# Layer 1's attention with the two query halves in the two row halves of the TensorE array

## The chip, the cores and the metric

The kernel runs on one NeuronCore of one Trainium2 chip, as one launch. The metric is the device time of that launch in microseconds (us), the median of several runs. Inside the core, five engines work side by side, each through its own instructions in order and with semaphores between them: TensorE (PE in the profile; its weight loads are listed apart as PEld), VectorE (DVE), ScalarE (ACT), GpSimd (POOL) and SyncE (SP), which here issues nearly all DMAs. Products are written to PSUM, eight banks of 512 float32 on each of 128 partitions.

## What is computed

Two layers of a transformer-like backbone over 1024 latent tokens and 256 context tokens of width 1024, batch 1, in float32. Layer 0 is grouped-query attention, layer 1 (the last one) multi-head latent attention with 16 heads. Only layer 1's attention is touched by the change. Cut to what matters, for each head, with 64 "nope" columns, 32 rotary columns that all heads share on the key side, and all 1280 keys:

```
s = (einsum("qd,kd->qk", q_nope, k_nope) + einsum("qr,kr->qk", q_rope, k_rope)) * 96 ** -0.5
p = softmax(s, axis=-1)
o = p @ v                      # 1024 queries x 64
y = (o * silu(g)) @ w_out      # all heads together, then x + gate * y
```

## The kernel before

**Precision.** Operands that need float32 accuracy are split into a high part (float32r, rounded) and a low part (what is left). A product is then the sum of high x high, high x low and low x high. For layer 1 the parts of queries and keys lie in DRAM: `q1h`, `q1l` (per head 96 rows: 64 nope, 32 rotary) and `k1h`, `k1l` (64 nope rows per head), `kr1h`, `kr1l` (32 rotary rows for all heads).

**The `Attention` class** serves both layers; each layer hands in a dictionary `ops` with its own functions. A *unit* is one head of latent queries (layer 0 has four more units for the context queries). Layer 1 has 16 units. A unit works through ten *key tiles* of 128 keys:

- `do_scores` (L422, L424): the scores of 128 keys (partitions) against 1024 queries go to a PSUM tile `st` of two banks, 512 queries in each. In layer 1 `l1_scores` gives three operand pairs, each used for both query halves: six products with 96 or 97 rows. The 97th row subtracts a shift for each query: the keys' row is -1, the queries' row (`crow`) is the row's maximum. ScalarE then writes `p`, the exponential, to SBUF.
- Between the products, `one_more` slips in the *maxima* of a later unit (`maxima`, `do_max`, L362 to L369): a product of high parts alone, 128 queries against 512 latent keys, or two products of 128 queries against 256 context keys, into a PSUM tile `mx` of one bank, and a VectorE reduction of that bank. A unit has 16 latent steps and 4 context steps; two steps come with each key tile.
- When a unit's maxima are complete, `do_shift` lines up a turn, which is run after the ten score tiles (`run_turns`): a transpose on TensorE, a copy on VectorE (L384), and a DMA that puts the row into its place beside the queries (L385).
- `add_up` (L445, POOL) and `pair_sum` (L431, DVE) sum the tiles of `p` for the softmax's denominator. `total` (L500 to L506) finishes that sum for the unit before, in the PSUM bank of that unit's `av`.
- `do_av` (L458): the product with V for all ten key tiles, two products of 64 columns for each, one for each query half, in the two column halves of the array. `p` and V are plain float32, so each is two instructions. `finish` copies the result out (L479).

`run` writes down this order for TensorE, VectorE and ScalarE by hand (`manual_schedule`); SP's and POOL's instructions are put in order by the framework. `start_unit` (from `run`, two units ahead) calls the layer's `load`: in layer 1 `l1_load` (L1382 to L1388), six DMAs and a memset of the -1 row, into `KH`, `KL`, `QH`, `QL` with three buffers each. PSUM during the loop: two banks `mx`, two tiles `st` of two banks, two banks `av`.

**Around it.** Before the loop the last eight gate slices of layer 1 run (`gate_slice`, 24 products each, L92 to L94); from the fourth slice on, six maxima steps come with each of four slices, 24 in all, ordered by the framework. `open_early` opens the pools for keys, queries and `mx` before the gate slices, `open_late` the others after them, in memory that the gate's operands leave. Then `run(24, 2, ...)`, then the output projection.

## Time and profile before

| what | value |
|---|---|
| runs | 1738.92, 1737.24 and 1739.38 us; median 1738.92 |
| the profiled execution, first to last instruction (span) | 1736.6 us, 2.3 us under the median |
| granted TensorE clock, mean | 0.997 |
| layer 1's attention loop | about 1197 to 1642 us from the span's start |
| gate slices with maxima before it | about 1168 to 1197 us |
| output projection after it | about 1642 to 1737 us |

The profile is one execution. Matmuls are pipelined: a matmul row's duration (0.39 us for 512 columns) reaches over its drain, so what a product costs TensorE is read from the distance of starts or from the chain of waits, not from the duration. Rows with "x2" or more are runs of like instructions merged, and their time is that of the whole run. A row's bracket tells how long the engine had been idle and who ended that. The chain of waits follows the work that ended last back from the end. The lines themselves stand where the prediction uses them.

### The profile page before, as it was taken

The page shows a single profiled execution, that of the slowest core. Times are in us where ns is not written, and L with a number is a line of the kernel's source. Part 1 is how long each engine was busy: PE and PEld are TensorE (multiplying, and loading weights), DVE is VectorE, ACT ScalarE, POOL GpSimd, SP SyncE. Part 2 cuts the span into 40 slices and gives each one's busy share as a digit, 9 for nine tenths or more (in the row PEclk, how much of TensorE's full clock was granted, in tenths as well). Part 3 has the DMA queues.
Part 4 walks back from the last instruction along what each step waited for, and adds up shares of the span by engine and source line. Part 5 has one row for each costly group of instructions (what it writes and reads, how often), then busy time and mean ns, then how long its engine had stood idle before and what let it go on. Part 6 is the DMA issues. An engine that isn't in the chain of part 4 may idle for free. (4 is left out here: it accounts for less than half of the span.)

```text
span 1736.6 us, 23794 instructions
## 1 busy us (share of the span) xinstructions
PE 1703.1 (98%) x8548; PEld 1232.5 (71%) x8548; DVE 1068.4 (62%) x1807; ACT 644.5 (37%) x943; POOL 979.5 (56%) x657
## 2 busy tenths in 40 slices
PE   8999999999999999999989999999999999999998
PEld 5776778776655665558878798978666666657587
DVE  3765651368777877625575667756676767667231
ACT  4632221134544544433244633332343443434310
POOL 2763430237888897752344644443587878777511
PEclk9999999999999999999999999999999999999999
DMA  9457854432332422156434857685434443441452
GB/s 326 156 160 235 265 167 136 133 98 55 100 91 71 116 66 74 44 145 189 137 94 132 238 163 199 181 234 162 104 88 118 108 104 91 111 112 43 118 162 73
DMA packets 211901, 234.33 MB, mean 135 GB/s; under 512 B 20680, under 2 KB 157880, under 8 KB 211784
## 3 DMA queue, kind: packets, MB, share of 16 engines
q1 hardware_dynamic: 211360, 232.71, 47.2%
q8 instruction: 67, 1.10, 0.3%
q14 instruction: 50, 0.41, 0.1%
q10 hardware_dynamic: 424, 0.11, 0.0%
HBM read 158.98 MB, written 73.63 MB: 134 GB/s over the span
## 5 line engine op out<-in xcount | busy, mean ns | idle before, releaser
L363 DVE TENSOR_REDUCE m<-mx 128x1 f32<-128x512 f32 x512 | 351.5, 691 | 203.6 <-PE mx L362 201.5
L424 ACT ACTIVATE p<-st 128x1024 f32<-128x1024 f32 x328 | 335.3, 1024 | 219.5 <-PE st L422 185.1
L445 POOL TENSOR_TENSOR acp<-acp,p 128x1024 f32<-128x1024 f32 x128 | 305.7, 2388 | 8.7
L458 PE MATMUL av<-p,v 128*64 128x512 f32 x1312 | 289.9, 595 | 0.0
L458 PEld LDWEIGHTS av<-p,v 128*64 128x64 f32 x1312 | 90.8, 137 | 181.0 <-issue 178.6
L445 POOL TENSOR_TENSOR acp<-p 128x1024 f32<-128x1024 f32 x34 | 81.3, 2391 | 168.3 <-ACT p L424 167.9
L445 POOL TENSOR_TENSOR acp<-acp,acd 128x1024 f32<-128x1024 f32 x60 | 141.5, 2358 | 22.2 <-DVE acd L431 19.4
L431 DVE TENSOR_REDUCE acd<-p 128x512 f32<-128x1024 f32 x124 | 144.6, 1219 | 7.7 <-ACT p L424 7.7
L135 POOL TENSOR_TENSOR wb<-wraw,wa 128x512 fp32r<-128x512 f32 (+3 forms) x73 | 95.5, 1324 | 90.6 <-ACT wa L156 90.0
L92 PE MATMUL mm<-wa,hh 128*128 128x512 f32 (+2 forms) x336 | 127.3, 379 | 1.7 <-ACT hh L787 1.7
L422 PE MATMUL st<-QH,KL 96*128 96x512 f32 x320 | 123.5, 392 | 0.0
L94 PE MATMUL mm<-wa,hl 128*128 128x512 f32 (+2 forms) x336 | 121.3, 361 | 1.4 <-DVE hl L790 1.4
L93 PE MATMUL mm<-wb,hh 128*128 128x512 f32 (+2 forms) x336 | 120.9, 360 | 0.0
L479 ACT COPY os<-av 128x512 f32<-128x512 f32 x36 | 21.1, 586 | 252.9 <-PE av L458 173.5
L369 DVE TENSOR_REDUCE m<-mx 128x2 f32<-128x512 f32 x144 | 99.3, 692 | 25.3 <-PE mx L367 24.4
L92 PE MATMUL y<-wa,oh 128*128 128x512 f32 (+1 forms) x296 | 114.1, 386 | 0.0
L93 PE MATMUL y<-wb,oh 128*128 128x512 f32 (+1 forms) x296 | 113.6, 384 | 0.0
L94 PE MATMUL y<-wa,ol 128*128 128x512 f32 (+1 forms) x296 | 113.6, 384 | 0.0
L422 PE MATMUL st<-QA,KA 128*128 128x512 f32 x336 | 106.6, 399 | 0.7 <-ACT p L424 0.7
L422 PE MATMUL st<-QB,KB 65*128 65x512 f32 x336 | 105.5, 395 | 0.0
L362 PE MATMUL mx<-KA,QA 128*128 128x512 f32 x256 | 102.4, 405 | 1.2 <-DVE m L363 1.0
L362 PE MATMUL mx<-KH,QH 96*128 96x512 f32 x256 | 102.3, 401 | 0.0
(232 smaller groups left out, 3423.4 us busy)
## 6 DMA issues: line engine op xcount, KB each, us to landing
mraw<-in_l_w_mod SPq DMA_DIRECT2D x64, 256.0 KB
wraw<-in_l_w_in SPq DMA_DIRECT2D x28, 512.0 KB
rb<-rrow SPq DMA_DIRECT2D x72, 128.0 KB
mraw<-in_l_w_mod SPq DMA_DIRECT2D x16, 512.0 KB
sgd<-gth SPq DMA_DIRECT2D x32, 256.0 KB
QA<-q0h SPq DMA_DIRECT2D x32, 256.0 KB
wraw<-in_l_w_out SPq DMA_DIRECT2D x16, 512.0 KB
sg<-sgd SPq DMA_DIRECT2D x64, 128.0 KB
```

What stands on the lines that cost most here:

```text
L92: pe.matmul(ps, lhsT=lh(k), rhs=rh(k), start=first and i == 0, stop=False)
L93: pe.matmul(ps, lhsT=lh(k), rhs=rl(k), start=False, stop=False)
L94: pe.matmul(ps, lhsT=ll(k), rhs=rh(k), start=False, stop=last and i == len(ks) - 1)
L135: eng.tensor_sub(lo, a, b)
L362: pe.matmul(m, lhsT=s["mq"][:, i * P:(i + 1) * P], rhs=s["mk"][:, n * 512:(n + 1) * 512], start=True, stop=True)
L363: dve.reduce_max(s["m"][:, i, n:n + 1], m, axis=AX.X)
L369: dve.reduce_max(s["m"][:, 2 * i:2 * i + 2, 2 if u["kind"] == "lat" else 0], m.rearrange("p (a b) -> p a b", a=2), axis=AX.X)
L422: pe.matmul(ps[:, n * 512:(n + 1) * 512], lhsT=lh, rhs=rf(n), start=(j == 0), stop=(j == len(prods) - 1))
L424: act.activation(p, ps, AF.Exp, scale=self.ops["scale"])
L431: dve.reduce_sum(t[:, ns], p2.rearrange("p a n -> p n a")[:, ns, :], axis=AX.X)
L445: pool.tensor_add(t, a, b)
L458: pe.matmul(s["av"][64 * n:64 * n + 64, :], lhsT=s["v"][:, kt, u["vc"]:u["vc"] + 64], rhs=p[:, n * 512:(n + 1) * 512], start=kt == kts[0], ...
```

## The change

A constant `HALVES = (False, True)` switches a second form of the attention on for layer 1 alone. (The diff also carries functions for layer 0, which are not called.)

- **Scores** (`scores_by_halves`, `l1_scores` with `n`): query half 0 lives on partitions 0 to 63, half 1 on partitions 64 to 127, so a product of one half has 64 rows and lies in one row half of the array. Keys are held twice, once in each half. The sum over 96 columns and three precision parts is cut into five steps of 64 rows (the last of 33), issued for the two halves in turn: high x high, low x high and high x low of the nope part; then 32 + 32 rows with the rotary keys' high and low parts against the queries' high part twice; then 32 rows of rotary high against the queries' low part with the shift row as the 33rd.
- **Maxima** (`max_parts`, `next_maxima`, `side_by_side`): the same 16 + 4 steps a unit, each of two products of 64 rows (nope, rotary) for one query half. Two steps, one of each half, go with a key tile: half 0's ahead of its scores, half 1's after three of its scores. A latent step is two parts, taken in turn with the other half's products; a context step issues its four products of 256 columns at once (`part_ctx`).
- **PSUM**: three banks `mx`, two tiles `st`, one bank `av`; `total` takes an `mx` tile.
- **Loads** (`l1_load_halves`): `KH`, `QH`, `QR` with three buffers when a unit is started, eight DMAs; `rest` loads `KL`, `QL`, `QS` with two buffers, six DMAs, for unit t+2 after the last scores of unit t. `KR` is filled once in `open_early`, `KS` with its -1 rows in `open_late`. The shift row goes out in two DMAs, and its SBUF tile has one buffer instead of two, in layer 0 too. The pool of the gate slices before the loop has two buffers instead of four.

The diff, cut:

```
+HALVES = (False, True)
...
-            self.ps_m = st.enter_context(tc.tile_pool(name=f"psm{l}", bufs=2, space=PSUM, side="right", reuse_waits="tile"))
+            self.ps_m = st.enter_context(tc.tile_pool(name=f"psm{l}", bufs=3 if HALVES[l] else 2, space=PSUM, side="right", reuse_waits="tile"))
+            if HALVES[l]:
+                self.ops["open"](self, st)
...
+                bufs = 1 if HALVES[l] and name == "ps_o" else 2
...
+        def max_parts(self, u, step):
...
+            def part(j):
+                if j == 0:
+                    held["m"] = self.ps_m.tile([P, 512], F32, name="mx", tag="mx")
+                pairs = self.ops["maxima"](s, half)
+                q, k = pairs[j]
+                for t, ks, cs in spans:
+                    pe.matmul(held["m"][:, cs], lhsT=q[:, t * P:(t + 1) * P], rhs=k[:, ks], start=j == 0, stop=j == len(pairs) - 1)
+                if j == len(pairs) - 1:
+                    dve.reduce_max(s["m"][:, i, n:n + 1], held["m"], axis=AX.X)
+
+            def part_ctx():
+                held["m"] = self.ps_m.tile([P, 512], F32, name="mx", tag="mx")
+                m = held["m"]
+                pairs = self.ops["maxima"](s, half)
+                for t, ks, cs in spans:
+                    for j, (q, k) in enumerate(pairs):
+                        pe.matmul(m[:, cs], lhsT=q[:, t * P:(t + 1) * P], rhs=k[:, ks], start=j == 0, stop=j == len(pairs) - 1)
+                dve.reduce_max(s["m"][:, 2 * i:2 * i + 2, 2 if u["kind"] == "lat" else 0],
+                               m.rearrange("p (a b) -> p a b", a=2), axis=AX.X)
+
+            if kind == "ctx":
+                return half, [part_ctx] + [lambda: None] * (self.ops["mparts"] - 1)
+            return half, [lambda j=j: part(j) for j in range(self.ops["mparts"])]
...
-                r = self.sm.tile([8, P], F32R, name="crow", tag="crow", bufs=2)
+                r = self.sm.tile([8, P], F32R, name="crow", tag="crow", bufs=1)
...
+                    for n in range(2):
+                        sp.dma_start(raw(s["crow"][n]), raw(r[4 * n:4 * n + 4, :]))
...
+            if "rest" in s and self.started < 2:
+                s.pop("rest")()
+            if HALVES[self.l]:
+                if lat:
+                    self.todo += [(u, ("lat", i + 4 * a, n)) for i in range(4) for n in range(2) for a in range(2)]
+                self.todo += [(u, ("ctx", i + 2 * a, 0)) for i in range(2) for a in range(2)]
...
+        def side_by_side(*streams):
+
+            for t in range(max(map(len, streams))):
+                for stream in streams:
+                    if t < len(stream):
+                        stream[t]()
...
+            if HALVES[self.l]:
+                steps = self.next_maxima(upto, limit)
+                self.side_by_side(*([f for half, parts in steps if half == a for f in parts] for a in range(2)))
+                return
...
+        def scores_by_halves(self, u, kt, p, steps):
+
+            s = self.state[id(u)]
+            ps = self.ps_s.tile([P, 1024], F32, name="st", tag="st")
+            prods = [self.ops["scores"](s, kt, n) for n in range(2)]
+            last = len(prods[0]) - 1
+
+            def product(j, n):
+                lh, rh = prods[n][j]
+                pe.matmul(ps[:, n * 512:(n + 1) * 512], lhsT=lh, rhs=rh, start=j == 0, stop=j == last)
+
+            streams = [[lambda j=j, n=n: product(j, n) for j in range(last + 1)] for n in range(2)]
+            for half, parts in steps:
+                at_ = (last + 2) // 2 if half else 0
+                streams[half][at_:at_] = parts
+            self.side_by_side(*streams)
+            act.activation(p, ps, AF.Exp, scale=self.ops["scale"])
...
-                t = s["av"] if u is not self.units[-1] else self.ps_m.tile([P, 512], F32, name="mx", tag="mx")
+                t = s["av"] if u is not self.units[-1] and not HALVES[l] else self.ps_m.tile([P, 512], F32, name="mx", tag="mx")
...
+                            if HALVES[self.l]:
+                                count += 2
+                                self.scores_by_halves(u, kt, ps[i], self.next_maxima(count, t + 1 + ahead))
...
+                        if end and t + 2 < self.started:
+                            self.state[id(self.units[t + 2])].pop("rest", lambda: None)()
...
+    def l1_open(at, st):
+        at.KR = st.enter_context(tc.tile_pool(name="rope1", bufs=1, **right)).tile([P, NT], F32R, name="KR")
+        for n in range(2):
+            sp.dma_start(raw(at.KR[64 * n:64 * n + 32, :]), kr1h)
+            sp.dma_start(raw(at.KR[64 * n + 32:64 * n + 64, :]), kr1l)
+
+    def l1_open_late(at, st):
+        at.KS = st.enter_context(tc.tile_pool(name="rope1s", bufs=1, reuse_waits="tile")).tile([P, NT], F32R, name="KS")
+        for n in range(2):
+            pool.memset(raw(at.KS[64 * n + 32:64 * n + 33, :]), -1.0)
+            sp.dma_start(raw(at.KS[64 * n:64 * n + 32, :]), kr1h)
+
+    def l1_load_halves(u, at):
...
+        halves = [(64 * n, slice(512 * n, 512 * n + 512)) for n in range(2)]
+        for b, cs in halves:
+            sp.dma_start(raw(KH[b:b + 64, :]), k1h[h // 2, r, :])
+            sp.dma_start(raw(QH[b:b + 64, :]), q1h[h, 0:64, cs])
+            for o in (0, 32):
+                sp.dma_start(raw(QR[b + o:b + o + 32, :]), q1h[h, 64:96, cs])
+
+        def rest():
+            KL = kp.tile([P, NT], F32R, name="KL", tag="KL", bufs=2)
+            QL = qp.tile([P, 512], F32R, name="QL", tag="QL", bufs=2)
+            QS = qp.tile([P, 512], F32R, name="QS", tag="QS", bufs=2)
+            for b, cs in halves:
+                sp.dma_start(raw(KL[b:b + 64, :]), k1l[h // 2, r, :])
+                sp.dma_start(raw(QL[b:b + 64, :]), q1l[h, 0:64, cs])
+                sp.dma_start(raw(QS[b:b + 32, :]), q1l[h, 64:96, cs])
+            s.update(KL=KL, QL=QL, QS=QS, crow=[QS[b + 32:b + 33, :] for b, _ in halves])
...
+    def l1_maxima(s, n):
+        r = slice(64 * n, 64 * n + 64)
+        return [(s["QH"][r, :], s["KH"][r, :]), (s["QR"][r, :], s["KR"][r, :])]
...
+    def l1_scores(s, kt, n=None):
         ks = slice(kt * P, (kt + 1) * P)
+        if n is not None:
+            r = slice(64 * n, 64 * n + 64)
+            r33 = slice(64 * n, 64 * n + 33)
+            return [(s["KH"][r, ks], s["QH"][r, :]), (s["KL"][r, ks], s["QH"][r, :]), (s["KH"][r, ks], s["QL"][r, :]),
+                    (s["KR"][r, ks], s["QR"][r, :]), (at.KS[r33, ks], s["QS"][r33, :])]
...
-    with tc.tile_pool(name="wkg1", bufs=4, **right) as wkg:
+    with tc.tile_pool(name="wkg1", bufs=2 if HALVES[1] else 4, **right) as wkg:
```

More of the change, by code (lines that the diff above doesn't have):

```diff
@@ L369, in do_max @@
                 dve.reduce_max(s["m"][:, 2 * i:2 * i + 2, 2 if u["kind"] == "lat" else 0], m.rearrange("p (a b) -> p a b", a=2), axis=AX.X)
+        def max_parts(self, u, step):
+            s = self.state[id(u)]
+            kind, i, n = step
+            if kind == "lat":
+                half, spans = i // 4, [(i % 4, slice(n * 512, n * 512 + 512), slice(0, 512))]
+            else:
+                half, spans = i // 2, [(2 * (i % 2) + a, slice(NL, NT), slice(a * 256, a * 256 + 256)) for a in range(2)]
+            held = {}
+            def part(j):
[19 more added lines that the diff above has]
+            return half, [lambda j=j: part(j) for j in range(self.ops["mparts"])]
         def do_shift(self, u):
@@ L1156, in hybrid_kernel @@
         units.insert(pos, ctxu[g])
-    at = Attention(0, units, dict(scale=0.125, load=l0_load, scores=l0_scores, kbufs=2, qbufs=3, vw=256))
+    at = Attention(0, units, dict(scale=0.125, load=l0_load, scores=l0_scores, maxima=l0_maxima, mparts=1, open=l0_open, kbufs=2, qbufs=3, vw=256))
     stE = ExitStack()
@@ L1402, in hybrid_kernel @@
                               kts=list(range(TT))))
-    at = Attention(1, units, dict(scale=float(96 ** -0.5), load=l1_load, scores=l1_scores,
+    at = Attention(1, units, dict(scale=float(96 ** -0.5), load=l1_load, scores=l1_scores, maxima=l1_maxima, mparts=2, open=l1_open, open_late=l1_open_late,
                                   kbufs=3, qbufs=3, vw=128))
```

97 lines of the change are left out of this document (84 added, 13 removed).

## The prediction

> **What bounds the kernel now.** I read the page's totals first, then the busy time by windows, then the chain of waits inside layer 1's attention, then single pieces of that chain.
>
> ```profile
> span 1736.6 us, 23794 instructions
> ...
> PE 1703.1 (98%) x8548; PEld 1232.5 (71%) x8548; DVE 1068.4 (62%) x1807; ACT 644.5 (37%) x943; POOL 979.5 (56%) x657
> ```
>
> ```profile
> 1168.00:1197.00 29.00, 29.00 (x129) 22.78 (x128) 18.50 (x30) 3.53 (x6) 2.54 (x2) 1.00 0.72 206
> 1197.00:1642.00 445.00, 445.00 (x2092) 285.85 (x2090) 291.14 (x419) 179.59 (x187) 324.43 (x161) 1.00 0.39 97
> ```
>
> The two windows are the end of the gate stage and the attention loop of layer 1. In the loop TensorE is busy in all 445 us at full granted clock (1.00), VectorE in 291, GpSimd in 324, ScalarE in 180, the DMA engines in 0.39. The chain agrees that nothing but TensorE's own order sets the pace:
>
> ```profile
> by line: PE st L422 50.7%; PE av L458 29.8%; PE mx L362 13.9%; PE mx L367 3.5%; PE av L500 1.8%; PE mx L382 0.4%; PE mm L94 0.1%
> ```
>
> So time saved on TensorE in this loop is saved from the span, until another engine is late. The change touches the scores (st) and the maxima (mx), not the product with V (av). Pieces of the chain in order of time:
>
> ```profile
> 1207.26 0.23 PE mx L362
> 1207.49 0.70 PE st L422 x3
> 1208.20 0.25 PE mx L367 x2
> 1208.44 0.70 PE st L422 x3
> ...
> 1215.76 8.73 PE av L458 x40
> ```
>
> One product of 512 columns takes a slot of 0.232 us (0.70 / 3), one of 256 columns 0.12 (0.25 / 2). A key tile is six score products and two steps of the maxima: 8 x 0.232 = 1.855 us, or 1.87 where the steps are those over the context keys (4 products of 256 columns). How many of each kind:
>
> ```profile
> L363 DVE TENSOR_REDUCE m<-mx 128x1 f32<-128x512 f32 x236 | 163.2, 691 | 110.3 <-PE mx L362 109.9
> L369 DVE TENSOR_REDUCE m<-mx 128x2 f32<-128x512 f32 x60 | 41.5, 692 | 14.7 <-PE mx L367 14.7
> L424 ACT ACTIVATE p<-st 128x1024 f32<-128x1024 f32 x160 | 163.8, 1024 | 143.4 <-PE st L422 118.3 <-DVE m L369 12.5 <-DVE m L363 11.4
> ```
>
> Two reductions stand in a key tile: 236 / 2 = 118 latent tiles, 60 / 2 = 30 context tiles, and of 160 tiles 12 have none (the last units), at 6 x 0.232 = 1.39 us.
>
> **The change, part by part.**
>
> *Scores.* Six products of 512 columns become ten of 64 (once 33) rows, in pairs that sit in different row halves and write different banks. If a pair takes the slot of one product, that is five slots. No row of this trace shows two row halves at work. The nearest is two column halves, the product with V:
>
> ```profile
> L214 PE MATMUL tp<-modrow,fold x8: 591/591/592, 131.1 to 238.8; 128*2 128x512 f32 x8
> 131.13 1.02 PE L214 MATMUL tp<-modrow,fold 128*2 128x512 f32 x2
> ```
>
> L214 is two passes of 512 float columns with no partner: 1.02 - 0.591 = 0.43 us from start to start. The 40 passes of av, in pairs of column halves, take 8.73 us: 0.437 a pair. There a pair costs what one costs alone. I therefore take **0.232 us for a pair of row halves**, the slot of the same float32r product. Bounds: below, 0.437 / 2 = 0.218 (the av stream at the same number of columns; float32r's own extra over it would vanish). Above, the weights: each product of a pair has its own load of 128 columns, and the closest thing to two loads in a slot is the pair of 256-column products, 0.25 us.
>
> A weight load starts now together with the product before it, on the same rows, and is over before that product's slot is:
>
> ```profile
> 1403.66 0.39 PE L422 MATMUL st<-QH,KL 96*128 96x512 f32 x1
> 1403.67 0.19 PEld L362 LDWEIGHTS mx<-KH,QH 96*128 96x128 f32 x1
> 1403.89 0.39 PE L362 MATMUL mx<-KH,QH 96*128 96x512 f32 x1
> ```
>
> So I count no load beside the slot. [...]
>
> With 0.232: a latent tile is 7 slots (two products of a maximum in one half beside two score products in the other), 1.62 us, so 0.232 x 118 = **-27.4**. A tile without maxima saves one slot: 12 x 0.232 = **-2.8**. A context tile is different: `part_ctx` issues its four 256-column products in one go in one half, and products start in the order of the program in every row here, so three of the four run alone in each half. By hand: 3 x 0.12, then six slots (two score products of half 1 come first, the second beside half 0's first), with the other half's 3 x 0.12 among them: 0.72 + 1.39 = 2.11 us against 1.87, 30 x 0.24 = **+7.2**. Together -23.0. By 0.218 (0.11 for the short ones): -(1.855 - 1.526) x 118 - (1.39 - 1.09) x 12 + (1.97 - 1.87) x 30 = -39.4. By 0.25 (0.125): -0.105 x 118 - 0.14 x 12 + (2.25 - 1.87) x 30 = -2.7.
>
> *What comes next when TensorE is faster.* In a latent tile of 1.62 us VectorE has 2 x 0.691 = 1.38, ScalarE 1.02. Both still fit, VectorE with little room; the third mx buffer keeps it off TensorE's way. GpSimd's 324 us are 20.3 of 27.8 a unit and lose a memset a unit. Cost 0; below 1.4 us a tile VectorE would be the bound.
>
> *The maxima in the gate stage.* 24 steps run there among 128-row products. In the present timeline they stand singly or in twos, about five visits in each of four gate slices, the first and last:
>
> ```profile
> 1168.45 0.70 PE L362 MATMUL mx<-KH,QH 96*128 96x512 f32 x2
> ...
> 1193.77 0.40 PE L362 MATMUL mx<-KH,QH 96*128 96x512 f32 x1
> ```
>
> Afterwards each visit changes the array between whole and halved rows. Such a change can be seen where av ends:
>
> ```profile
> 1420.83 0.14 PEld L458 LDWEIGHTS av<-p,v 128*64 128x64 f32 x2 [0.28 <-issue]
> 1421.78 0.19 PEld L362 LDWEIGHTS mx<-KH,QH 96*128 96x128 f32 x1 [0.81 <-issue]
> 1421.78 0.50 PE L362 MATMUL mx<-KH,QH 96*128 96x512 f32 x1
> 1422.12 0.62 PE L422 MATMUL st<-QL,KH 96*128 96x512 f32 x2
> ```
>
> The first weights come only with the product, and the next product starts 0.34 after it instead of 0.23; with some 0.09 before it, 0.2 us a change. With pairs, ten visits x 2 changes x 0.2 = **+4** (0 if they bunch, 8 for twenty visits). In the loop the number of changes stays: the totals and av are in column tiles already.
>
> *The loads.* `KS` is filled in `open_late`, where memory becomes free with the last gate product, and the fifth step of the first tile needs it. v, loaded at that moment now, shows when:
>
> ```profile
> 1197.10 0.38 SPq L352 DMA_DIRECT2D v<-vd  x1
> 1197.14 0.63 PE L422 MATMUL st<-QL,KH 96*128 96x512 f32 x2
> ...
> 1615.94 1.11 SPq L516 DMA_DIRECT2D rb<-rrow  x2
> 1619.63 1.29 POOL L519 TENSOR_TENSOR rb<-rb,sg 128x512 f32<-128x512 f32 x1 [3.11 <-DMA rb<-rrow]
> ```
>
> rb landed 3.7 us after its first issue. KS, issued at about 1197.5, is there at 1201.2; the fifth step would be due at 1198.5: **+2.7**, once (0 to 5). KL, QL and QS of unit t+2 are asked for at the end of unit t and have a whole unit. A unit issues 14 loads instead of 7 and moves 2.2 MB instead of 1.7 (tile sizes in the code); at 0.4 to 0.7 us an issue (rows here) and a DMA share of 0.39 neither is near its end. The shift row follows them on SP's queue: six issues of about 0.5 us and 1 MB stand ahead of its two.
>
> ```profile
> 1413.02 0.69 SPq L385 DMA_DIRECT2D QH<-crow  x1
> ```
>
> It is issued at 1413.0, its unit's first product starts at 1421.8: nearly 9 us of cover, of which the six issues take 3 and the megabyte some 4 (97 GB/s at a share of 0.39 make 250 GB/s). Cost 0, and if the cover goes, a wait of TensorE at the fifth step of each unit. The totals move from av's bank to an mx buffer, held through the 8.7 us of av, when no maxima run: 0; so av can do with one bank. In layer 0 only one thing changes, one crow buffer instead of two: where two heads end together VectorE waits for a DMA under the cover of av: 0.
>
> **Sum:** -23.0 + 4 + 2.7 = -16.3 us. The execution of the trace (span 1736.6) becomes 1720.3; the median of the runs shown lies 2.3 above that span, so **1722.6 us**.
>
> **The rivals.**
>
> *Weight loads in a row* (slower). If the two loads of a pair follow each other at 0.125, the slot is 0.25: -2.7 + 6.7 = +4.0, **1742.9 us**. It decides from a slot of 0.246, where gain and the 6.7 us cancel. For it: 14 loads in a latent tile, and loads with almost no product between come at 0.10 us each, (0.95 - 0.25) / 7 here:
>
> ```profile
> 192.38 0.95 PE L221 MATMUL tp<-fold,modrow 128*128 128x2 f32 x8
> ```
>
> Against it: av's two loads of 64 columns lie in 0.14 us, the length of one.
>
> *Loads not under the products of their own half.* Then a slot is 0.232 + 0.10 = 0.332 and a short product 0.22: 0.469 x 118 + 0.27 x 12 + 1.44 x 30 = +102, with 6.7 **1847 us**. Against it: the rows at 1403.66, where it does not happen. It decides from the same slot of 0.246, that is, as soon as 0.014 us of a load stand free. [...]
>
> *No pairing at all:* 14 slots, 3.25 us a latent tile. 1.39 x 118 + 0.93 x 12 + 1.41 x 30 = +218, with 6.7 **1964 us**. The change would not do what it says. Only av's pairs speak against it.
>
> *The shift row late:* 2 us a unit beyond its cover, 15 x 2 = +30 on the forecast: **1753 us**. The DMA share of 0.39 speaks against it.
>
> **How the numbers follow.** Forecast (a pair in less than 0.243 us) 0.64; weight loads in a row 0.17; loads not covered 0.08; no pairing 0.05; shift row late 0.06. A measurement of this kernel can tell about 0.2% (3.5 us) from no change. The forecast is faster: 0.64. Of the rival of 0.25, 0.10 lies within 3.5 us and 0.07 above; with the other three, slower 0.26. The range begins at slot 0.218 with no changes of mode to pay, 1738.9 - 39.4 + 2.7 = 1702, and a little lower, 1700, for KS unseen; it ends at 1753, which takes in the weight loads with 8 us of changes and the late shift row. Outside lie the two dear rivals, 0.13, and a little of the rest.
>
> **What would show it.** Right: starts of paired st products with hardly any distance, ACT's exp every 1.62 us in latent tiles and about 2.1 in context tiles, av still 8.7. A wait for KS near the loop's start, about 3 us. Exp every 1.75 us or more with weight loads one behind the other means the first rival; 2.3 the second; 3.2 the third. A gap before each unit's fifth step that ends with a crow DMA means the fourth. Wrong altogether: VectorE or GpSimd ending TensorE's waits.

## The result, and the profile after

The changed kernel takes 1726.99 us (median of 4 runs, 1726.58 to 1727.77), beside 1738.47 for the kernel before on the same chip: a ratio of 0.9935, 95% interval 0.9921 to 0.9949. The prediction was 1722.6 in a range of 1700 to 1753.

The page's totals of the changed kernel, then its two stretches by windows (columns after the length: PE, PEld, DVE, ACT, POOL busy with instructions, granted clock, DMA share, GB/s):

```profile
span 1724.7 us, 26057 instructions
...
PE 1685.1 (98%) x9572; PEld 1226.2 (71%) x9572; DVE 1069.4 (62%) x1807; ACT 644.9 (37%) x943; POOL 963.5 (56%) x643
```

```profile
1150.00:1219.00 69.00, 64.14 (x252) 43.72 (x251) 25.01 (x40) 10.56 (x19) 11.20 (x9) 0.93 0.62 165
1219.00:1628.00 409.00, 408.92 (x3064) 274.54 (x3066) 286.77 (x414) 177.48 (x184) 306.59 (x147) 1.00 0.53 123
```

In the loop TensorE is still busy in all but 0.1 of 409 us, so it is still the bound; but the loop starts later, after a stretch with 5 us of idle time and a mean clock of 0.93. Where the time went is best read from one group of instructions that both kernels have, the 160 exps of layer 1's loop. The rows give the first and the last start, the kernel before first:

```profile
L424 ACT ACTIVATE p<-st x160: 1023/1024/1028, 1199.0 to 1638.7; 128x1024 f32<-128x1024 f32 x160
```

```profile
L508 ACT ACTIVATE p<-st x160: 1024/1027/1033, 1219.5 to 1626.8; 128x1024 f32<-128x1024 f32 x160
```

From first to last exp: 439.7 us before, 407.3 after, **32.4 us won in the loop**. The first exp starts at 1219.5 instead of 1199.0, **20.5 us lost on the way to it**. After the last exp both kernels need 97.9 us to the end of the span. So 20.5 - 32.4 = -11.9, which is the difference of the spans (1724.7 - 1736.6).

**The loop.** The products of one latent key tile and the start of the next, changed kernel, from the timeline of TensorE:

```profile
1401.49 0.39 PE L393 MATMUL mx<-KH,QH 64*128 64x512 f32 x1
1401.49 0.39 PE L501 MATMUL st<-QH,KH 64*128 64x512 f32 x1
1401.72 0.39 PE L393 MATMUL mx<-KR,QR 64*128 64x512 f32 x1
...
1403.11 0.39 PE L393 MATMUL mx<-KH,QH 64*128 64x512 f32 x1
```

The two products of a pair start together, the next pair 0.23 later, the next tile 1.62 after this one: seven slots of 0.232, as the prediction had it. A context tile is what it did not foresee:

```profile
1383.54 0.28 PE L403 MATMUL mx<-KH,QH 64*128 64x256 f32 x1
1383.55 0.49 PE L501 MATMUL st<-QH,KH 64*128 64x512 f32 x1
1383.66 0.28 PE L403 MATMUL mx<-KR,QR 64*128 64x256 f32 x1
1383.78 0.28 PE L403 MATMUL mx<-KH,QH 64*128 64x256 f32 x1
1383.88 0.39 PE L501 MATMUL st<-QH,KL 64*128 64x512 f32 x1
1383.90 0.28 PE L403 MATMUL mx<-KR,QR 64*128 64x256 f32 x1
...
1385.20 0.28 PE L403 MATMUL mx<-KH,QH 64*128 64x256 f32 x1
```

In the program all four short products (L403) stand ahead of the first st product. On the chip half 1's st product starts 0.01 after the first short one and half 1 goes on to its second at 1383.88, while half 0 is still at its short ones. In these rows the order of the program holds within a row half, not across the two. The tile takes 1385.20 - 1383.54 = 1.66 us, not the 2.11 that was worked out for it.

**The entry.** Idle times of TensorE and the granted clock there, changed kernel; the rows are from its timeline (the bracket is the idle time before the product and who ended it) and from windows of 10 us:

```profile
1169.28 0.50 PE L393 MATMUL mx<-KH,QH 64*128 64x512 f32 x1
1171.83 0.47 PE L393 MATMUL mx<-KH,QH 64*128 64x512 f32 x1 [2.05 <-DMA QH<-q1h]
...
1215.82 0.50 PE L501 MATMUL st<-QH,KH 64*128 64x512 f32 x1 [0.98 <-DVE gth L303]
1219.03 0.47 PE L501 MATMUL st<-QS,KS 33*128 33x512 f32 x1 [1.52 <-DMA KS<-kr1h]
```

```profile
1160.00:1170.00 10.00, 9.78 (x43) 7.59 (x41) 1.38 (x2) 2.24 (x4) 2.54 (x2) 1.00 0.96 261
1170.00:1180.00 10.00, 8.15 (x17) 3.92 (x18) 4.28 (x7) 0.60 (x1) 0.00 (x0) 0.64 0.87 210
1180.00:1190.00 10.00, 10.00 (x36) 6.68 (x34) 3.44 (x7) 0.60 (x1) 0.00 (x0) 0.85 0.22 71
```

```profile
1182.66 0.43 PE mm L95
...
1183.38 0.23 PE mm L94
...
1185.87 1.13 PE mx L393 x6
...
1188.13 0.66 PE mx L393 x2
1188.79 0.44 PE mm L94
1189.22 0.66 PE mx L393 x2
...
1195.27 1.13 PE mx L393 x6
```

TensorE waits 2.05 us for `QH`, while the DMA share is 0.96; after that the gate products come 0.43 us apart until 1183, then 0.23 (last fence, the chain of waits). A *visit* is a group of maxima products between gate products. A visit of one maxima step takes 0.66 and the gate product after it 0.44: its two products lie in one row half, so nothing pairs with them. Only the first visit of a slice, six products in 1.13, holds a pair (the timeline has two products each at 1185.80 and 1186.13, then two single ones). At the loop's start TensorE waits 0.98 for a PSUM bank that the last gate slice leaves, and 1.52 for `KS`.

### The profile page after: what moved, and what is told of

It is laid out like the page before. It is cut to its first block, busy times and chain, and to the rows that moved or that the text cites. A ratio compares the mean times of both kernels' runs of the same rounds, so it can differ in the third digit from the quotient of the medians.

```text
span 1724.7 us, 26057 instructions
## 1 busy us (share of the span) xinstructions
PE 1685.1 (98%) x9572; PEld 1226.2 (71%) x9572; DVE 1069.4 (62%) x1807; ACT 644.9 (37%) x943; POOL 963.5 (56%) x643
## 5 line engine op out<-in xcount | busy, mean ns | idle before, releaser
L501 PE MATMUL st<-QH,KH 64*128 64x512 f32 x320 | 121.9, 404 | 1.0 <-DVE gth L303 1.0
L501 PE MATMUL st<-QH,KL 64*128 64x512 f32 x320 | 118.6, 392 | 0.0
L501 PE MATMUL st<-QL,KH 64*128 64x512 f32 x320 | 118.0, 390 | 0.0
```

The source lines that it names most:

```text
L501: pe.matmul(ps[:, n * 512:(n + 1) * 512], lhsT=lh, rhs=rh, start=j == 0, stop=j == last)
```

## The experiments

Theory A of the result: the loop wins what the pairs promise and more, since the halves run each at its own pace; what is missing is lost at the entry, to loads that are late, to the clock after a wait, and to maxima that run unpaired. The rivals are named with each run. Times are medians; "span" is that of the profiled run.

### Does the order of the program bind the halves?

```
-            self.side_by_side(*streams)
+            for f in streams[0] + streams[1]:
+                f()
```

> All products of query half 0 of a key tile are issued before those of half 1; nothing else differs. Theory A (each row half takes its own products in order and passes the other half's, as the context tiles of the changed kernel suggest): the halves still overlap; a latent tile takes 1.6 to 2.3 us (more than 1.63 only because half 0 runs ahead and must wait for a st tile), the whole 1727 to 1840 us. Theory B (products start in program order): 14 slots of 0.232 one after the other, 3.2 us a tile, about 1980 us.

One run alone: 1755.54 us. The exps, from the timeline of ScalarE:

```profile
1417.04 1.03 ACT L509 ACTIVATE p<-st 128x1024 f32<-128x1024 f32 x1 [2.03 <-PE st L501]
1418.61 1.03 ACT L509 ACTIVATE p<-st 128x1024 f32<-128x1024 f32 x1 [0.55 <-PE st L501]
1420.44 1.03 ACT L509 ACTIVATE p<-st 128x1024 f32<-128x1024 f32 x1 [0.80 <-PE st L501]
```

Tiles take 1.57 and 1.83 us in turn, 1.70 in the mean, though all of half 0 is issued ahead of all of half 1. Products that start in the order of the program, Theory B, would make them 14 slots, 3.2 us. So the halves overlap with all of half 0 issued first too. This is what the context tiles showed. Written in turn they are still 0.08 us a tile better, so the order isn't free of cost. Over whole units it costs more: the ten exps of the unit that begins at 1417.04 span 15.5 us instead of 14.7, the step from one unit's last exp to the next unit's first takes 12.2 instead of 11.4, and from first to last exp it is 433.9 us instead of 407.3.

### What the late `QH` costs

The maxima begin one gate slice later, with eight steps in each of three slices instead of six in four:

```
-            if 2 < at.step < len(todo_g) - 1:
-                at.maxima(at.done + 6, 2)
+            if 3 < at.step < len(todo_g) - 1:
+                at.maxima(at.done + 8, 2)
```

> The 24 maxima of the gate stage come with the last three slices before the end (8 each) instead of four (6 each), so the first one comes about 5.6 us later and finds its queries loaded. Theory A (the wait of 2.05 us for QH, and the half clock of some 11 us that follows it, cost about 9 us): no wait, granted clock 1.00 in the stage, 1717 us. Theory B (the clock falls because the array is switched between whole and halved rows): the clock still falls, at most 2 us are gained, 1725 us or more.

1725.25 us (1722.91 to 1726.78), ratio to the kernel before 0.9917 (0.9904 to 0.9931), span 1721.1. The wait for `QH` is gone and the clock is 1.00 in every window from 1160 to 1210; the first exp starts 5.1 us sooner, at 1214.4. At the loop's start the waits for the bank (0.98) and for `KS` (1.69) stay, and now the clock drops there, to 0.83:

```profile
1210.00:1220.00 10.00, 7.73 (x51) 6.99 (x53) 5.16 (x8) 2.80 (x3) 3.79 (x3) 0.83 0.95 243
```

The clock stayed up although the array still changes between whole and halved rows at every visit, so Theory B's cause is out, though its time came true. The size that Theory A gave was wrong: 3.6 us of span, in the fastest of five runs, and 1.7 between the medians. The waits at the loop's start took a part back. By the intervals of the ratios this kernel can't be told from the changed one; the same holds for each repair of layer 1 below, up to and with the kernel that joins two of them.

### What unpaired maxima cost

TensorE's order in the gate stage is written out by hand, and a callback between the gate products issues two steps at a time, one of each half, so that they pair; three visits a slice.

```
+        def pair(i):
+            if 2 < at.step and i in (1, 4, 7) and at.done < 24:
+                at.maxima(at.done + 2, 2)
+        with in_order(mybir.EngineType.PE):
```

> In the gate stage TensorE's order is written out: maxima come two steps at a time, one of each half, their four products side by side, three such visits in each of four slices. Theory A (in the changed kernel a visit there has both parts of one half after each other, so nothing is paired, 0.23 us a step, and there are more visits, each with two changes of mode): a slice takes 8.2 us instead of 9.4, about 5 us in all; the wait for QH and the half clock stay; 1722 us. Theory B (the wait and the clock are all that was lost there): within 2 us of the changed kernel, 1725 to 1728 us.

1724.95 us (1722.38 to 1726.44), ratio 0.9911 (0.9898 to 0.9925), span 1724.3. A visit of two steps (four products) takes the 0.66 us that one step took, and a slice takes 8.12 us (1180.19 to 1188.31 in the chain), near the 8.2 of Theory A, instead of 9.40. But the load came later in this order, and TensorE waited for `QH` twice:

```profile
1172.44 0.72 PE L393 MATMUL mx<-KH,QH 64*128 64x512 f32 x1 [2.98 <-DMA QH<-q1h]
1175.25 0.76 PE L393 MATMUL mx<-KH,QH 64*128 64x512 f32 x1 [2.08 <-DMA QH<-q1h]
```

The time that the pairs save went into that wait: the first exp starts at 1219.1, 0.4 sooner than with the change as it was.

### Both layers

`HALVES = (True, True)`: layer 0's attention in row halves too.

> The second form is switched on for layer 0 too: there a score is 4 steps of 64 rows instead of 2 products of 128, the same number of slots, but two maxima steps take one slot instead of two: 5 slots instead of 6 a tile, 1.16 us against 1.39. Theory A (VectorE's two reductions, 1.38 us, become the bound): a tile still takes 1.38 to 1.42 us, layer 0's loop of about 400 us is the same within 1%, and its gate stage loses some us as layer 1's did: 1727 to 1745 us. Theory B (TensorE alone sets the pace): 1.2 us a tile, some 30 us less: 1695 to 1710 us.

One run alone: 1712.74 us, span 1710.9, which neither theory had. Layer 0's exps come two in 2.60 us (1.30 a tile), against two in 2.81 with the change as it was:

```profile
520.15 2.12 ACT L508 ACTIVATE p<-st 128x1024 f32<-128x1024 f32 x2 [0.47 <-PE st L501]
522.75 2.14 ACT L508 ACTIVATE p<-st 128x1024 f32<-128x1024 f32 x2 [0.48 <-PE st L501]
```

```profile
521.65 2.48 DVE L404 TENSOR_REDUCE m<-mx 128x2 f32<-128x512 f32 x4
524.04 2.67 DVE L395 TENSOR_REDUCE m<-mx 128x1 f32<-128x512 f32 x4
```

VectorE's rows stand one behind the other with hardly a gap, two reductions a tile, and with that the 1.38 us a tile that the expectation took from single rows is no bound: four reductions take 2.48 us. But VectorE is not what TensorE waits for. The list of waits between 400 and 740 us, for the weight loads of TensorE, has

```profile
PEld st L501 <- ACT p L508: 20.3, 59, 0.7
```

as its longest wait for another engine: 59 waits for ScalarE's exp, 20.3 us in all (1.7 us in four with the change as it was). For VectorE's reductions only the turn at a unit's end waits, 5.4 us in all. A tile `st` has two buffers, so the first product of a tile needs the exp of the tile two before it to be over: the exp that starts at 520.15 ends at 521.18, and that product starts at 521.23. Two tiles then take the products of one (1.43 us with the drain), its exp (1.03) and two short steps of 0.09 and 0.05: 2.60 us. This is read from the rows; a third buffer was not tried.

### Is it the issue of `KS` or its transfer?

```
-            sp.dma_start(raw(at.KS[64 * n:64 * n + 32, :]), kr1h)
+            act.dma_start(raw(at.KS[64 * n:64 * n + 32, :]), kr1h)
```

> The two loads of KS are issued from ScalarE's queue instead of SP's; nothing else. Theory A (at the loop's start the second KS load stands behind SP's store of the last gate slice, and TensorE waits 1.52 us for it): both KS loads are issued within about 0.5 us of the memory becoming free, KS lands some 1.5 us sooner, the wait before the fifth score product falls from 1.52 to 0.5 us or less, time 1727.0 - 1.5 = 1725.5 us. Theory B (the transfer itself, or the memory's release, sets the moment of landing): the wait stays within 0.3 us of 1.52 and the time at 1727.0.

Theory B. The second half's fifth step waits 1.46 us for it still, and the first half's now waits 1.32, which the profile puts down to no one. The two loads are issued at 1208.4 and 1208.9, right after each other, and the second half is there at 1215.01, about 6 us later; in the changed kernel the second load is issued at 1216.19 and is there at 1219.03, 2.8 later. SP asks for v at 1208.44, so v is now ahead of the second half, where it was 0.5 us behind it; whether this makes the transfer longer is not shown by any run.

```profile
1212.79 0.76 PE L501 MATMUL st<-QS,KS 33*128 33x512 f32 x1 [1.32 <-issue]
1215.01 0.76 PE L501 MATMUL st<-QS,KS 33*128 33x512 f32 x1 [1.46 <-DMA KS<-kr1h]
```

1730.0 us (1724.54 to 1736.03, ratio 0.9951, 0.9931 to 0.9970): no gain that can be told from the changed kernel. The profiled run, the fastest of six, has a span of 1722.8 for a reason that was not edited: in it the first `QH` is only 0.73 us late, the clock stays at 1.00 until 1210, and the first st product starts at 1209.81, 6.0 us sooner than in the changed kernel. So the late `QH` and the clock after it cost about 6 us, and how late it is differs between executions of nearly the same program. The spread of the six runs is not explained.

### The entry put right, one part at a time

The next kernel joins the two repairs: order by hand, four visits of two steps in each of the last three slices, `KS` from ScalarE's queue.

> Layer 1 alone, as in the change, but the maxima ahead of the loop stand in the last three gate slices only, in four visits of two units' steps each, written out between the gate products so that the two row halves follow each other closely; KS loads from ScalarE. Theory A (the entry cost 18.7 us and the KS wait 1.5, made of a 2.05 us wait for QH with a lower clock after it, of maxima that run unpaired, and of the changes of mode): no wait of TensorE for QH, granted clock 1.00 from 1160 to 1210, slices with maxima 9.0 us each (4.0 us of gate products plus 12 steps at 0.4 us or less), KS wait under 0.5 us; the entry is 9 us shorter than the changed kernel's and the loop as long as there: 1727.0 - 9 = 1718 us. Theory B (what is lost at the entry is the low clock, which comes with the change between row halves and whole array, not with the wait): the clock falls again in the slices, and the time is 1723 us or more.

1722.96 us (1721.05 to 1727.62), ratio 0.9915 (0.9900 to 0.9929), span 1721.1. The slices run as expected, a visit every 2.25 us (two gate steps of 0.68 and 0.89 for the visit with its two changes of mode), and the first st product starts at 1207.87 instead of 1215.82. A wait of 1.42 us for the first `QH` is still there, with a clock of 0.83 after it, which was not expected. And the loop's fifth steps wait 1.78 and 1.51 us for `KS`, and the clock is 0.66 in the window after 1210: the first exp comes at 1214.4, no sooner than with the maxima merely begun later. Of the 8 us won ahead of the loop, 2.9 went into the next waits and 1.5 more into the slow clock after the first exp. The time is the one that Theory B named, but not by its cause: with the same visits the clock is 1.00 from 1180 to 1210, and it is low only behind the waits. With both layers:

> The previous kernel's entry with both layers' attention in row halves. Theory A (gains of separate stages add): 1712.7 (both layers, looked at once) - 9 = 1704 us; layer 0's tile stays at 1.29 to 1.30 us, set by VectorE's two reductions, not by TensorE's 1.04 to 1.2. Theory B (layer 0 gains nothing more than its tile, and its own entry is dearer because its maxima too run unpaired): the same time as layer 1 alone minus 14 us in any case, but then the loop of layer 0 starts at 374 us or later, 5 us behind the kernel before, as it did in the look at both layers.

1706.63 us (1706.21 to 1709.5), ratio 0.9818 (0.9806 to 0.9831), span 1707.7: 13.4 us of span between the last two kernels (the profiled run is the slowest of four; the medians differ by 16.3), near the 14 that were expected. Layer 0's first exp starts at 373.4, 4.3 behind the kernel before's 369.1: its entry is dearer too, though not the full 5 us of Theory B, and its loop wins more than that, 375.0 us from first to last exp instead of 392.0.

Then `KS` without a transfer. `KR` holds the same rows on the same partitions, so two copies on the chip replace the two loads:

```
-            act.dma_start(raw(at.KS[64 * n:64 * n + 32, :]), kr1h)
+            (act.copy, dve.tensor_copy)[n](at.KS[64 * n:64 * n + 32, :], raw(at.KR[64 * n:64 * n + 32, :]))
```

> The entry kernel (1722.96 us, span 1721.1) with one edit: the 32 rows of KS in each half are copied on the chip from the same rows of KR, which hold the same values, by ScalarE and VectorE, so KS needs no transfer. Theory A (KS sets the start of the loop: in the entry kernel the two fifth score products wait 1.78 and 1.51 us, and the low clock after it costs about 1.7): the fifth products start by 1209.6 (there 1211.31 and 1213.58), clock 1.00 from 1210 to 1220, 5 us less: 1718 us. Theory B (the second unit's QH and QR, issued at 1208.24 and 1208.78 behind SP's store of the last gate slice, are as late as KS): TensorE waits for QH or QR until 1212 or later, the gain is 1.5 us or less, 1721.5 us or more.

**1714.5 us** (1713.78 to 1717.98), ratio 0.9854 (0.9839 to 0.9869), span 1711.9. Theory A, and more than it said. The timeline of TensorE, and the clock:

```profile
1204.80 0.50 PE L501 MATMUL st<-QH,KH 64*128 64x512 f32 x1 [1.20 <-DVE gth L303]
...
1206.06 0.83 PE L501 MATMUL st<-QS,KS 33*128 33x512 f32 x2
```

```profile
1210.00:1220.00 10.00, 10.00 (x96) 9.09 (x94) 8.60 (x14) 6.18 (x7) 9.69 (x5) 1.00 0.60 175
```

The fifth steps run from 1206.06 without an idle time of TensorE before them, and the clock stays at 1.00. Of the 9.2 us of span between this kernel and the entry kernel, 3.1 lie ahead of the first score (1204.80 for 1207.87: the first `QH` was 0.2 us late this time, not 1.42, and the clock stayed up), 4.4 between it and the first exp (2.1 for 6.5: the waits for `KS`), and 1.5 after it (the slow clock there). The last two, 5.9 us, are the copy's, about the 5 of Theory A. The 3.1 come before `KS` is needed, and no run shows that they are the copy's too. From first to last exp it is 407.3 us, as in the changed kernel: the 12.8 us of span between those two were won ahead of the loop, all but 0.2 of them.

### The store's place

Two edits at once: the gate slices' stores go out from ScalarE's queue, and the first visit comes later in its slice (three, four and five visits in the last three slices instead of four in each).

> The previous kernel with the gate slices of this stage stored from ScalarE's queue, so that SP's loads of the second unit stand behind no store, and with the first visit of the maxima three gate steps later in its slice. Theory A: no wait of TensorE over 1 us between 1160 and 1230 apart from the bank of the last gate slice (0.98), clock 1.00 in all of it, the first wait for QH (1.42) gone: 1721.1 - 5 - 3 = span 1713, time 1715 us. Theory B (the loads are late because the DMA engines are full, not because of their place on the queue): a wait for QH or QR of 1.5 us or more stays at the loop's start, and the time is 1718 us or more.

Neither theory: 1717.02 us (1714.8 to 1719.53), ratio 0.9864 (0.9846 to 0.9882), span 1715.8, 3.9 more than without. The clock is 1.00 throughout and the wait for `QH` is 0.98 us, as Theory A has it, but the gain did not come. The same with both layers:

> The previous kernel with both layers' attention in row halves. There the wait before the loop of layer 1 was 1.64 + 1.99 us, ended by QR, with a clock of 0.76 after it, and no wait for the first QH. Theory A: that wait goes with the store's move and the copy, 5 us: 1706.6 - 5 = 1701.5 us. Theory B: as for the previous kernel, 1705 us or more.

1700.86 us (1698.2 to 1701.74), ratio 0.9769 (0.9755 to 0.9784), as Theory A has it: no wait for `QR` is left. To part the two edits, the store's move alone, and the copy alone with both layers:

```
-        sp.dma_start(sgd[l][4 * c + m, :, s0:s0 + n], th[:, :n])
+        (q or sp).dma_start(sgd[l][4 * c + m, :, s0:s0 + n], th[:, :n])
```

> The kernel that copies KS (1714.5 us, span 1711.9), with the stores of the gate slices issued by ScalarE and the visits of the maxima left where they were. It tells the two edits of the missed step apart. Theory A (the store's move set SP's queue otherwise: its weight load came ahead of KH and QH, which were asked for at 1167.28 instead of 1163.19): the loads are as late here, TensorE waits for QH 3 us or more, span about 1715. Theory B (the later visits cost it: less of the last slices stands without maxima): span 1712, KH asked for by 1164.

> The kernel that copies KS, with both layers' attention in row halves and SP's stores left where they were. Theory A (the copy alone brings all of the gain at the start of layer 1's loop, as it did with one layer, 1721.1 to 1711.9): span 1707.7 - 7.5 (the difference of the first exp's start there) = 1700, time 1702 us, the same as with the store's move within 0.2%. Theory B (with both layers the wait before the loop was for QR, behind SP's store, so the copy alone does not help): a wait of 1.5 us or more for QR or QH stays, 1705 us or more.

The store's move alone: 1722.04 us (1719.29 to 1723.17), ratio 0.9895 (0.9879 to 0.9911), span 1721.4, worse still. Theory B is out: the later visits were no part of the loss, since with them the span is 1715.8 and without 1721.4. The loads are late, as Theory A says (`KH` is asked for at 1169.42 instead of 1163.19), but the wait for `QH` is 2.30 us instead of 3, and the span is 6 us over Theory A's. SP's rows and, from 1150 to 1176 us, its waits (us in all, times, longest), first of the kernel with the copy alone, then with the store moved:

```profile
1163.19 0.46 SPq L1541 DMA_DIRECT2D KH<-k1h  x1
```

```profile
SPq L1541 <- DMA q1h<-th: 2.4, 1, 2.4
```

```profile
1163.92 3.11 SPq L153 DMA_DIRECT2D wraw<-in_l_w_out  x2
1169.42 0.46 SPq L1541 DMA_DIRECT2D KH<-k1h  x1
```

```profile
SPq L1542 <- DMA wraw<-in_l_w_out: 1.5, 1, 1.5
SPq L1541 <- DMA q1h<-th: 1.2, 1, 1.2
```

The first `KH` does not wait for the weight load `wraw` ahead of it: in both kernels its issue waits for the stores of `q1h` and `q1l` to land, and these are later here because all that comes before them is. The first maximum starts at 1175.90 instead of 1170.10, with the same gate products before it, so 5.8 of the 9.5 us of span are lost earlier: layer 0's last exp already comes 2.1 us later, and the rest lies between it and the gate slices. Why was not traced. What the queue's new order is seen to cost is the second half's `QH`: its issue waits 1.5 us for a `wraw` load, TensorE waits 2.30 us, and the clock falls to 0.83. These make the other 3.7 us.

Both layers with the copy and SP's stores left alone: **1699.46 us** (1698.46 to 1701.11), ratio 0.9770 (0.9755 to 0.9784), the fastest of all, as Theory A has it, and with the store moved it is the same within the intervals. It beats both kernels: 2.3% under the kernel before.

### The kernels by the exps of layer 1

| kernel | first exp | last exp | between | span |
|---|---|---|---|---|
| before | 1199.0 | 1638.7 | 439.7 | 1736.6 |
| changed | 1219.5 | 1626.8 | 407.3 | 1724.7 |
| one half after the other | 1221.9 | 1655.8 | 433.9 | 1753.8 |
| maxima later | 1214.4 | 1623.2 | 408.8 | 1721.1 |
| paired by hand | 1219.1 | 1626.4 | 407.3 | 1724.3 |
| `KS` from ScalarE | 1215.8 | 1624.8 | 409.0 | 1722.8 |
| paired, later, `KS` from ScalarE | 1214.4 | 1623.2 | 408.8 | 1721.1 |
| the same, `KS` copied | 1206.9 | 1614.2 | 407.3 | 1711.9 |
| `KS` copied, store moved, visits later | 1210.6 | 1617.9 | 407.3 | 1715.8 |
| `KS` copied, store moved | 1216.4 | 1623.7 | 407.3 | 1721.4 |
| both layers, as the change | 1205.9 | 1613.1 | 407.2 | 1710.9 |
| both layers, paired, later, `KS` from ScalarE | 1200.7 | 1609.9 | 409.2 | 1707.7 |
| both layers, `KS` copied, store moved, visits later | 1194.2 | 1601.5 | 407.3 | 1699.1 |
| both layers, paired, later, `KS` copied | 1192.8 | 1600.0 | 407.2 | 1697.7 |

With the halves in turn the loop is 407.2 or 407.3 us wherever the clock is full at its start, and 1.5 to 1.9 more where it is not. Everything else in the column of spans is when it starts.

## Why the prediction was right in sum, and where it was wrong

**What bounds, and that a faster TensorE shortens the loop: right.** With maxima beside the scores no other engine ends TensorE's waits in the loop; VectorE's 1.38 of a tile of 1.62 fits, as was said. That VectorE would be the bound below 1.4 us a tile is not borne out: at 1.30, in layer 0 in row halves, TensorE waits for ScalarE's exps.

**The slot of a pair, 0.232: right.** Seven slots give 1.62 us, av takes 8.73 us as before. With it the rival of weight loads in a row falls (exp every 1.75 or more), that of loads that stand free (2.3), and that of no pairing (3.2). A slot of 0.232, with a load in each half, is no longer than that of one product was (0.70 / 3).

**The context tile, +7.2: wrong, by about 14 us.** The step that failed is "products start in the order of the program in every row here". It was true of every row of a kernel whose products lay in the same rows, or in pairs of equal length; it says nothing of two streams of unequal length. With 1.66 us instead of 1.87 the 30 context tiles bring -6.3 instead of +7.2. The loop's terms then add to -27.4 - 2.8 - 6.3 = -36.5; measured are -32.4. The distances of the exps show where the other 4.1 us are. In a full unit the nine distances between its ten exps go from 16.67 us (1254.84 to 1271.51) to 14.70 (1271.23 to 1285.93), 1.97 saved where about 2.04 were due. The tenth, across av to the next unit's first exp, goes from 11.52 to 11.43, 0.09 where a tile's 0.23 was due. That is 0.2 a unit, some 3 us in all, most of it at the units' ends, and the chain of waits shows a part of it in the turn:

```profile
1390.34 0.20 PE mx L422
...
1391.11 8.73 PE av L555 x40
```

It takes 0.20 where it took 0.11. The rest is in the tiles without maxima at the end: six that follow each other (first exp 1609.50, last 1615.80) come 1.26 us apart in the mean, not the 1.16 of five slots, alternately after 1.1 and 1.5, and the weight loads there wait three times for ScalarE's exp, 1.4 us in all, as in layer 0.

The rows from 1383.55 to 1383.90 and the run with one half after the other (1.70 us a tile, not 3.2) show that here the order of the program did not hold between products in different row halves.

**The gate stage, +4: the size was wrong.** It counted only changes of mode, with ten visits, and took it for granted that the maxima pair there as in the loop. Mostly they did not: but for one pair a slice, the framework's order puts both products of a step one behind the other. From the rows: with 9.40 us between the maxima at 1185.87 and those a slice later at 1195.27, where the kernel before takes 7.1 (1168.45 to 1175.57), an entry slice loses 2.3; four of them some 9. The slice of 8.12 with paired visits parts this: 1.3 a slice for the pairing, some 5 in all, and 1.0 for the changes of mode, some 4. The kernel with paired visits and the copy of `KS` shows what the term is when nothing else is wrong: a visit costs 0.89 us, 12 x 0.89 = 10.7; the same 24 steps and their changes took 28.7 - 96 x 0.227 = 6.9 in the kernel before (first maximum to first score, less 96 gate products of 0.227). The difference is 3.8, which is the +4 of the prediction. A visit's two pairs are 0.46 of its 0.89, so a change of mode costs 0.21: its price was right, and the pairing was the miss. (The number of visits was not right, 12 paired ones instead of ten; what the kernel before loses at its own visits makes up for it.)

**What the prediction did not have at all:** the wait for `QH` (2.05 us) and the clock after it (the first slice, 1171.83 to 1185.87, takes 14.0 us, 4.6 more than the next). It asked whether the loads have room in the loop, not whether those of the first unit, eight now ahead of its maxima, are there for the first of them, at a moment when the DMA share was 0.96. The rows of SP, before and changed, show how much later they are asked for:

```profile
1156.66 0.47 SPq L1385 DMA_DIRECT2D QH<-q1h  x1
```

```profile
1166.31 0.75 SPq L1542 DMA_DIRECT2D QH<-q1h  x1
```

The first maximum starts at 1168.45 before and at 1169.28 in the changed kernel, so `QH` has 11.8 us there and its second half 3.0 here. In the changed kernel SP waits 2.0 and 0.5 us for the stores of `q1h` and `q1l` to land before it issues the first `KH`, and both loads of `QH` stand behind that. And the wait for the bank (0.98 us) was not seen.

**`KS`, +2.7: the mechanism was right,** 1.52 us measured. The range for it, 0 to 5, held; but it depends on what comes before: once the entry is shorter it is 1.78 + 1.51 with a clock of 0.66 behind it, and the copy took all of it away.

**Layer 0's one crow buffer, 0: not quite.** VectorE waits four times, 9.3 us in all, longest the row here. From first to last exp layer 0 takes 393.5 us instead of 392.0 (393.3 to 394.3 in the other runs with layer 0 in its old form), and 0.8 us is left at layer 1's first maximum (1169.28 against 1168.45). No run has the two buffers back, so that the buffer is the cause is not shown.

```profile
430.84 0.28 DVE L424 CAST crow<-mx 8x128 fp32r<-8x128 f32 x1 [2.56 <-DMA QB<-crow]
```

**The shift row, 0: right;** no fifth step waits in the loop. (A unit's loads went from six to 14, or with the shift row from seven to 16; the prediction set seven against 14.)

**The sum** came near because two errors had opposite signs: the loop gave 32.4 instead of 23.0, and the entry took 20.5 instead of 6.7. 9.4 us more were gained than forecast and 13.8 more lost. That the forecast of -16.3 lay 4.4 from the -11.9 measured is luck; the slot of a pair, the change of mode and `KS` are not.

## What to carry to other kernels

In these runs, work in the two row halves of the array was two streams: a context tile took 1.66 us where the prediction, by the order of the program, had 2.11, and a latent tile with one half issued after the other 1.70 where that order would have made 3.2. Cost such work by the longer stream, not by the order in which the two are written, and check for each stage that both streams have something to run, since products of one half alone paid their full slot here (a visit of one maxima step took 0.66 us, one of two steps in pairs the same 0.66). A faster loop is worth only what its entry leaves of it (32.4 us won, 20.5 lost): list every load and every buffer that the loop's first steps need, and look for values that are on the chip already before a load is moved to another queue. With the order that the framework made here, moving one DMA moved others (`KH` was asked for at 1169.42 instead of 1163.19 with the store moved); look at the whole queue again after each edit.

## What had not been expected of the hardware

- Products in different row halves started out of the program's order: half 1's first product starts at 1383.55, ahead of three of half 0's at 1383.66, 1383.78 and 1383.90 that the program has before it. A latent tile with one half issued after the other took 1.70 us instead of 1.62.
- The granted clock was lower after some of TensorE's waits and not after others. In windows of 10 us it was 0.64 after the 2.05 us for `QH` in the changed kernel, 0.83 after one wait of 1.42 us, after one of 1.69 and after one of 2.30, and 0.66 after 1.78 and 1.51 close together, after 1.32 and 1.46 and after 2.98 and 2.08. It did not fall after 0.2, 0.7 or 1.2, nor after the 1.52 for `KS` in the changed kernel. Where it is low in the changed kernel, it is 0.50 in every window of 0.5 us from 1173.0 to 1183.0, and the gate products come 0.43 us apart instead of 0.23; its two windows of 0.64 and 0.85 make 10.2 us at half clock. With 0.50 taken for the other runs too, 0.83 and 0.66 over 10 us are, as an estimate, some 3.4 and 6.8 us. No run shows what sets these lengths or why the clock fell after one wait and not after another.
- Reductions of 512 columns by VectorE, one behind the other, started 0.60 us apart (layer 0 in row halves: four in 2.48 us, the last one's row 0.68), though a single one has a row of 0.68 or 0.69.
